# Batched 64x64 matmul: results stored in 1 KB runs, evacuations by partition halves, b loads ungated

## The chip, the cores and the metric

The kernel runs on one core of a Trainium2 chip. The metric is the device time of one execution in microseconds (us); each version ran several times, beside runs of the kernel before on the same chip. Engines: PE (TensorE, matmuls), DVE (VectorE), ACT (ScalarE), POOL (GpSimd, issues DMAs), SP (issues DMAs).

## The reference

```python
# a, b: 1024 x 64 x 64, float32, normal random numbers
def reference(a, b):
    return np.matmul(a, b).astype(np.float32)
```

50.3 MB go through memory (16.8 MB each for a, b and the result). The arithmetic is in bf16.

## The kernel before

Work goes in 16 **turns** t of 64 matrices. Tiles of a hold 128 matrices, so that a new one is prepared every second turn (s = t // 2).

```python
    b_v = b.rearrange("(t g h) (kp u) n -> t (h kp) g (u n)", h=4, g=16, u=2)
    o_v = out.rearrange("(t g h) (mo w) n -> t (h mo) g (w n)", h=4, g=16, w=2)
    # ... pools: 5 result tiles, 4 PSUM banks for results (o_psum, bufs=4), 4 for transposes

    def multiply(t):                       # cut
        for gq in range(4):
            o_ps = o_psum.tile([128, 4, 2, 64], fp32, name="o_ps")
            # ... 16 matmuls into o_ps
            if last and gq % 2:
                nc.vector.tensor_copy(o_sb[:, gq, :, :, :], o_ps[:])
            else:
                nc.scalar.copy(o_sb[:, gq, :, :, :], o_ps[:])

        # ... the loop, cut
        for t in range(n_t):
            s, half = t // 2, t % 2
            if t + 1 < n_t:
                spread(t + 1)              # DVE: 4 copies, transposed a -> block-diagonal weights
            if half == 0:
                if s + 2 < n_s:
                    regroup(s + 2)         # DVE: 1 copy, loaded a -> order for the transposes
                # ... load_a
            multiply(t)                    # PE matmuls, evacuation PSUM -> SBUF
            if t + 1 < n_t:
                cast(t + 1)                # ACT: b to bf16
            # ... load_b
            if half == 0 and s + 1 < n_s:
                transpose(s + 1, 1)        # PE transposes, then copies on DVE and ACT
            if half == 1 and s + 2 < n_s:
                transpose(s + 2, 0)
            # ... store(t - 1)
```

The order in which the program names operations is the order of each engine's queue: in the trace of this kernel DVE starts its 94 memsets, copies and casts, and ACT its 95 copies and casts, in just that order.

## Time and profile before

| | before |
|---|---|
| time, median | 138.62 us (138.28 to 138.86, 4 runs) |
| span of the profile | 137.0 us |

To read this: busy shares say which engine works, and the waits say for whom the others stand still. Here the compute engines have slack (DVE is busy for 62% of the span, ACT for 57%), and ACT waits 16.1 us for result buffers that DMA empties. The prediction below shows these lines.

### The profile page before, as it was taken

What the parts mean: (1) busy time and instruction counts of PE and PEld (TensorE: products, weight loads), DVE (VectorE), ACT (ScalarE), POOL (GpSimd) and SP (SyncE); (2) the same over time, 40 slices, a digit from 0 to 9 for tenths busy, and PEclk for the clock granted to TensorE, in tenths of its full rate; (3) what the DMA queues carried; (4) which work ended last, traced back from release to release, by engine and by line L of the source; (5) the groups of instructions that cost most, each with busy time, mean ns of one, the idle gap of its engine ahead of it and who ended that gap; (6) DMA issues with size and microseconds to landing.
All of it is one profiled execution on the core that took longest, in us unless ns stands there. A gap on an engine that the chain in (4) does not pass through costs nothing.

```text
span 137.0 us, 2995 instructions
## 1 busy us (share of the span) xinstructions
PE 58.8 (43%) x1280; PEld 56.7 (41%) x1280; DVE 85.2 (62%) x94; ACT 77.5 (57%) x98; POOL 43.3 (32%) x57
## 2 busy tenths in 40 slices
PE   0000810685339746843075800957019645508100
PEld 0000800685239746853075800956019645507100
DVE  5772573670999899999449850699207867904200
ACT  0103280199907999970889209791297999715100
POOL 6932211422723452333113443430030330232600
PEclk9999996599955999999559995599955999995955
DMA  2999999999999999999999999999999999999992
GB/s 18 184 297 306 305 306 306 301 274 262 243 271 270 316 359 274 272 356 383 340 276 273 379 374 331 271 289 383 377 383 384 378 382 383 376 386 368 301 278 90
DMA packets 17469, 42.14 MB, mean 308 GB/s; under 512 B 1072, under 2 KB 1072, under 8 KB 17456
## 3 DMA queue, kind: packets, MB, share of 16 engines
q0 software_dynamic: 9008, 25.17, 66.7%
q1 hardware_dynamic: 7392, 14.68, 30.4%
q10 hardware_dynamic: 1056, 2.10, 4.0%
q8 instruction: 10, 0.16, 0.5%
q14 instruction: 3, 0.02, 0.0%
HBM read 33.55 MB, written 16.78 MB: 367 GB/s over the span
## 4 chain that ended last, share of the span: by engine, by line
DMA 57%; issue 25%; POOL 11%; POOLq 1%
DMA a_sb<-in_a_dram 40%; DMA out_dram<-o_sb 18%; POOL out_dram L147 6%; POOL a_sb L65 3%; POOL out_dram L141 2%; POOLq L244 1%; POOL identity L178 0%; POOL identity L64 0%; POOLq L147 0%; POOLq L178 0%; POOLq L141 0%; POOLq L65 0%; POOLq L233 0%
## 5 line engine op out<-in xcount | busy, mean ns | idle before, releaser
L157 PE MATMUL o_ps<-b_bf,at_bd 128*128 128x64 bf16 x1024 | 40.4, 208 | 45.9 <-ACT b_bf L121 37.9
L115 DVE COPY at_bd<-at_sb 32x2048 bf16<-32x2048 bf16 x64 | 46.9, 733 | 20.5 <-ACT at_sb L105 19.5
L157 PEld LDWEIGHTS <-at_bd 128*128 128x128 bf16 x1024 | 39.8, 108 | 47.4 <-issue 35.6
L169 ACT COPY o_sb<-o_ps 128x512 f32<-128x512 f32 x62 | 33.5, 614 | 25.7 <-DMA out_dram<-o_sb 16.1
L65 POOL DMA_DIRECT2D a_sb<-in_a_dram x32 | 20.9, 667 | 41.0 <-DMA a_sb<-in_a_dram 30.2
L147 POOL DMA_DIRECT2D out_dram<-o_sb x15 | 18.8, 1253 | 40.3 <-ACT o_sb L169 27.6
L97 PE MATMUL at_ps<-identity,a_bf 128*128 128x128 bf16 x256 | 20.6, 246 | 22.7 <-DVE a_bf L88 22.7
L121 ACT CAST b_bf<-b_sb 128x2048 bf16<-128x2048 f32 x15 | 29.1, 1942 | 0.0
L97 PEld LDWEIGHTS <-a_bf 128*128 128x128 bf16 x256 | 18.1, 113 | 23.1 <-DVE a_bf L88 23.1
L105 ACT COPY at_sb<-at_ps 128x1024 bf16<-128x1024 bf16 x16 | 16.7, 1047 | 11.3 <-PE at_ps L97 11.3
L103 DVE COPY at_sb<-at_ps 128x1024 bf16<-128x1024 bf16 x16 | 19.5, 1222 | 3.9 <-PE at_ps L97 3.5
L88 DVE COPY a_bf<-a_sb 128x4096 bf16<-128x4096 bf16 x8 | 10.2, 1278 | 10.2 <-DMA a_sb<-in_a_dram 10.0
L177 DVE MEMSET at_bd<- 128x4096 uint32 x2 | 6.9, 3472 | 2.5 <-PEq L233 1.7
L105 ACT ACT_TABLE_LOAD x1 | 1.3, 1283 | 6.7 <-issue 6.7
L141 POOL DMA_DIRECT2D out_dram<-o_sb x4 | 3.0, 755 | 4.4 <-ACT o_sb L169 4.0
L167 DVE COPY o_sb<-o_ps 128x512 f32<-128x512 f32 x2 | 1.4, 692 | 2.7 <-PE o_ps L157 2.7
L128 ACT CAST b_bf<-b_sb 128x512 bf16<-128x512 f32 x2 | 1.1, 616 | 2.9 <-DMA b_sb<-in_b_dram 2.9
L126 DVE CAST b_bf<-b_sb 128x512 bf16<-128x512 f32 x2 | 0.8, 424 | 3.2 <-DMA b_sb<-in_b_dram 3.2
L73 ACT MOVE_SHAPE b_sb<-in_b_dram x2 | 0.6, 320 | 3.2 <-POOL identity L64 2.2
L178 POOL TENSOR_SCALAR_AFFINE_SELECT identity<-identity 128x128 bf16<-128x128 bf16 x1 | 0.3, 349 | 0.0
L64 POOL MEMSET identity<- 128x128 bf16 x1 | 0.2, 224 | 0.0
L233 POOL MEMSET const-float32-0.0<- 128x1 f32 x1 | 0.1, 99 | 0.2 <-issue 0.2
(3 smaller groups left out, 0.3 us busy)
## 6 DMA issues: line engine op xcount, KB each, us to landing
out_dram<-o_sb POOLq DMA_DIRECT2D x15, 1024.0 KB, 21.0
a_sb<-in_a_dram POOLq DMA_DIRECT2D x32, 256.0 KB, 18.0
out_dram<-o_sb POOLq DMA_DIRECT2D x4, 256.0 KB, 7.6
b_sb<-in_b_dram SPq DMA_DIRECT2D x14, 0.5 KB, 20.6
b_sb<-in_b_dram ACTq DMA_DIRECT2D x2, 0.5 KB, 21.7
```

Of the source, the lines that this page charges most:

```text
L65: nc.gpsimd.dma_start(out=a_sb[:, h, :, :].rearrange("p v k -> p (v k)"), in_=a_v[s, h])
L88: nc.vector.tensor_copy(a_bf[:], a_sb[:].rearrange("p h v k -> p v h k"))
L97: nc.tensor.transpose(at_ps[:, vo, :], a_cols[:, 2 * vo + w, u::2], identity[:])
L103: nc.vector.tensor_copy(dst, src)
L105: nc.scalar.copy(dst, src)
L115: nc.vector.tensor_copy(bd_v[rows, :, :, h, :], at_v[rows, :, half, :])
L121: nc.scalar.copy(b_bf[:], b_sb[:])
L141: nc.gpsimd.dma_start(out=o_v[t, :, 4 * gq : 4 * gq + 4, :], in_=o_sb[:, gq, :, :, :].rearrange("p g w n -> p (g w n)"),)
L147: nc.gpsimd.dma_start(out=o_v[t], in_=o_sb[:].rearrange("p q g w n -> p (q g w n)"))
L157: nc.tensor.matmul(o_ps[:, g4, w, :], at_bd[:, (2 * w + u) * 16 + g, :, :].rearrange("p h mo -> p (h mo)"), b_bf[:, g, 64 * u : 64 * u + 6 ...
L169: nc.scalar.copy(o_sb[:, gq, :, :, :], o_ps[:])
L177: nc.vector.memset(bd[:], 0.0)
```

## The change

The intent is to make the runs of the result in memory 1 KB long, where they were 512 B, so that its stores cost less DMA time. A result row of the matmul now holds two row halves (wl), and eight matrices share the 128 partitions. Evacuations (the copies that move matmul results from PSUM to SBUF) then have to move halves of the partitions, and they double in number. PSUM tiles of results double in size and halve in number. The second intent is to start b's first loads without waiting for a's first one.

```diff
-    o_v = out.rearrange("(t g h) (mo w) n -> t (h mo) g (w n)", h=4, g=16, w=2)
+    o_v = out.rearrange("(t gh x) (mo w) n -> t (x mo) gh (w n)", gh=8, x=8, w=4)
 ...
-        tc.tile_pool(name="o_psum", bufs=4, space=bass.MemoryType.PSUM)
+        tc.tile_pool(name="o_psum", bufs=2, space=bass.MemoryType.PSUM)
 ...  (load_b: the dependency on the first load of a is gone for t < 2)
 ...  (at_sb, at_bd: axes in another order, and spread's copies with them)
 ...  (transpose: each copy out of the transposes cut in two, one for each wl)
-        for gq in range(4):
-            o_ps = o_psum.tile([128, 4, 2, 64], fp32, name="o_ps")
 ...
-                nc.scalar.copy(o_sb[:, gq, :, :, :], o_ps[:])
+        def evacuate(o_ps, gh, gl, n):
+            for par in range(2):
+                for wl in range(2):
+                    src = o_ps[64 * wl : 64 * wl + 64, gl : gl + n, par, :, :]
+                    dst = o_sb[64 * par : 64 * par + 64, gh : gh + n, :, wl, :]
+                    if wl == par or (gh and not last):
+                        nc.scalar.copy(dst, src)
+                    else:
+                        nc.vector.tensor_copy(dst, src)
+        for half in range(2):
+            o_ps = o_psum.tile([128, 4, 2, 2, 64], fp32, name="o_ps")
 ...  (32 matmuls)
+                if last and g8 % 4 == 3:
+                    evacuate(o_ps, 4 * half + g8 // 4 * 2, g8 // 4 * 2, 2)
+            if not last:
+                evacuate(o_ps, 4 * half, 0, 4)
```

In the built program the four copies of a first half wait for each other. The semaphore values of turn 0:

```text
ACT  copy (par 0, wl 0)   waits PE  >= 80     then ACT counter = 8
DVE  copy (par 0, wl 1)   waits ACT >= 8
DVE  copy (par 1, wl 0)                       then DVE counter = 21
ACT  copy (par 1, wl 1)   waits DVE >= 21
```

I call this the **ring**. I read the values from the built program.

More of the change, by code (lines that the diff above doesn't have):

```diff
@@ L5 @@
 from concourse import bass_utils, mybir
+from concourse.masks import make_identity
 from concourse._compat import with_exitstack
@@ L49 @@
     o_psum = ctx.enter_context(
-        tc.tile_pool(name="o_psum", bufs=4, space=bass.MemoryType.PSUM)
+        tc.tile_pool(name="o_psum", bufs=2, space=bass.MemoryType.PSUM)
     )
     bd_tiles = [
-        consts.tile([128, 64, 4, 32], bf16, name=f"at_bd{i}") for i in range(N_BD)
+        consts.tile([128, 4, 16, 2, 4, 16], bf16, name=f"at_bd{i}") for i in range(N_BD)
     ]
@@ L57 @@
     a_tiles, b_tiles, abf_tiles, at_tiles, bbf_tiles = {}, {}, {}, {}, {}
-    held, begun = {}, []
+    held = {}
     def load_a(s):
@@ L62, in load_a @@
         for h in range(4):
-            if s == 0 and h == 1:
-                begun.append(nc.gpsimd.memset(identity[:], 0.0))
             nc.gpsimd.dma_start(
@@ L72, in load_b @@
         queue = nc.scalar if t in (1, 3) else nc.sync
-        load = queue.dma_start(out=b_sb[:], in_=b_v[t])
-        if t < 2:
-            tc.add_manual_dep(
-                load.ins,
-                begun[0].ins.name,
-                mybir.DependencyInfo(
-                    mybir.DependencyClass.Sync, mybir.DependencyReason.DATA
-                ),
-                reason="first load of a goes ahead",
-            )
+        queue.dma_start(out=b_sb[:], in_=b_v[t])
         b_tiles[t] = b_sb
@@ L89, in regroup, with transpose @@
         abf_tiles[s] = a_bf
-        at_tiles[s] = work.tile([128, 2, 2, 128, 8], bf16, name="at_sb")
-    def transpose(s, w):
+        at_tiles[s] = work.tile([128, 2, 2, 32, 2, 4, 4], bf16, name="at_sb")
+    def transpose(s, j):
         a_cols = abf_tiles[s][:].rearrange("p v h k -> p v (h k)")
         for u in range(2):
-            at_ps = t_psum.tile([128, 8, 128], bf16, name="at_ps")
-            for vo in range(8):
-                nc.tensor.transpose(
-                    at_ps[:, vo, :], a_cols[:, 2 * vo + w, u::2], identity[:]
-                )
-            dst = at_tiles[s][:, w, u, :, :]
-            src = at_ps[:].rearrange("p vo q -> p q vo")
-            if u == 0:
-                nc.vector.tensor_copy(dst, src)
-            else:
-                nc.scalar.copy(dst, src)
+            at_ps = t_psum.tile([128, 2, 4, 128], bf16, name="at_ps")
+            for wl in range(2):
+                for vo in range(4):
+                    nc.tensor.transpose(
+                        at_ps[:, wl, vo, :],
+                        a_cols[:, 4 * vo + 2 * j + wl, u::2],
+                        identity[:],
+                    )
+            src = at_ps[:].rearrange("p wl vo (g mp) -> p wl g mp vo", mp=4)
+            for wl in range(2):
+                dst = at_tiles[s][:, j, u, :, wl, :, :]
+                if u == 0:
+                    nc.vector.tensor_copy(dst, src[:, wl])
+                else:
+                    nc.scalar.copy(dst, src[:, wl])
     def spread(t):
-        at_v = at_tiles[t // 2][:].rearrange(
-            "p w u (g mp) vo -> p (w u) g (mp vo)", g=32
-        )
         half = slice(16 * (t % 2), 16 * (t % 2) + 16)
-        bd_v = bd_tiles[t % N_BD][:].rearrange("p (wu g) h mo -> p wu g h mo", g=16)
+        bd = bd_tiles[t % N_BD]
         for h in range(4):
             rows = slice(32 * h, 32 * h + 32)
-            nc.vector.tensor_copy(bd_v[rows, :, :, h, :], at_v[rows, :, half, :])
+            src = at_tiles[t // 2][rows, :, :, half, :, :, :].rearrange(
+                "p j u g wl mp vo -> p (j u) (g wl) (mp vo)"
+            )
+            dst = bd[rows, :, :, :, h, :].rearrange("p ju g wl mo -> p ju (g wl) mo")
+            nc.vector.tensor_copy(dst, src)
     def cast(t):
@@ L137, in multiply, with put @@
         last = t == n_t - 1
-        o_sb = o_pool.tile([128, 4, 4, 2, 64], fp32, name="o_sb")
-        def put(gq):
+        o_sb = o_pool.tile([128, 8, 2, 2, 64], fp32, name="o_sb")
+        def put(lo, n):
             nc.gpsimd.dma_start(
-                out=o_v[t, :, 4 * gq : 4 * gq + 4, :],
-                in_=o_sb[:, gq, :, :, :].rearrange("p g w n -> p (g w n)"),
-            )
-        def put_all():
-            nc.gpsimd.dma_start(
-                out=o_v[t], in_=o_sb[:].rearrange("p q g w n -> p (q g w n)")
-            )
-        for gq in range(4):
-            o_ps = o_psum.tile([128, 4, 2, 64], fp32, name="o_ps")
-            for g4 in range(4):
-                g = 4 * gq + g4
-                for w in range(2):
+                out=o_v[t, :, lo : lo + n, :],
+                in_=o_sb[:, lo : lo + n].rearrange("p gh j wl n -> p (gh j wl n)"),
+            )
+        def evacuate(o_ps, gh, gl, n):
+            for par in range(2):
+                for wl in range(2):
+                    src = o_ps[64 * wl : 64 * wl + 64, gl : gl + n, par, :, :]
+                    dst = o_sb[64 * par : 64 * par + 64, gh : gh + n, :, wl, :]
+                    if wl == par or (gh and not last):
+                        nc.scalar.copy(dst, src)
+                    else:
+                        nc.vector.tensor_copy(dst, src)
+        for half in range(2):
+            o_ps = o_psum.tile([128, 4, 2, 2, 64], fp32, name="o_ps")
+            for g8 in range(8):
+                g = 8 * half + g8
+                for j in range(2):
                     for u in range(2):
                         nc.tensor.matmul(
-                            o_ps[:, g4, w, :],
-                            at_bd[:, (2 * w + u) * 16 + g, :, :].rearrange(
-                                "p h mo -> p (h mo)"
+                            o_ps[:, g8 // 2, g8 % 2, j, :],
+                            at_bd[:, 2 * j + u, g, :, :, :].rearrange(
+                                "p wl h mo -> p (wl h mo)"
                             ),
@@ L165, in multiply @@
                         )
-            if last and gq % 2:
-                nc.vector.tensor_copy(o_sb[:, gq, :, :, :], o_ps[:])
-            else:
-                nc.scalar.copy(o_sb[:, gq, :, :, :], o_ps[:])
-        held[t] = [lambda q=q: put(q) for q in range(4)] if last else [put_all]
+                if last and g8 % 4 == 3:
+                    evacuate(o_ps, 4 * half + g8 // 4 * 2, g8 // 4 * 2, 2)
+            if not last:
+                evacuate(o_ps, 4 * half, 0, 4)
+        if last:
+            held[t] = [lambda q=q: put(2 * q, 2) for q in range(4)]
+        else:
+            held[t] = [lambda: put(0, 8)]
     with tc.manual_schedule():
@@ L177 @@
             nc.vector.memset(bd[:], 0.0)
-        nc.gpsimd.affine_select(
-            out=identity[:],
-            in_=identity[:],
-            compare_op=mybir.AluOpType.not_equal,
-            fill=1.0,
-            base=0,
-            pattern=[[-1, 128]],
-            channel_multiplier=1,
-        )
+        make_identity(nc, identity)
         for s in range(1, A_AHEAD):
```

## The prediction

> **What bounds the kernel now.** I read the page's head first, then the DMA view of a late stretch, then the waits, then the timeline of ScalarE (ACT).
>
> The page: busy time by engine, and the 40 slices in tenths (clock and DMA).
>
> ```profile
> PE 58.8 (43%) x1280; PEld 56.7 (41%) x1280; DVE 85.2 (62%) x94; ACT 77.5 (57%) x98; POOL 43.3 (32%) x57
> ...
> PEclk9999996599955999999559995599955999995955
> DMA  2999999999999999999999999999999999999992
> ```
>
> No compute engine reaches two thirds, while the 16 DMA engines are full from the second slice to the last but one. The clock falls to 5 or 6 after pauses of TensorE (PE).
>
> The DMA view of 90 to 120 us (packets, MB, share of the 16 engines), when only b and results move:
>
> ```profile
> q0 software_dynamic: 1960, 7.27, 66.9%
> q1 hardware_dynamic: 1959, 3.90, 35.6%
> ```
>
> Results (q0) and b (q1) together take 102%: both queues always have work. Results cost 0.669 x 30 x 16 / 7.27 = 44 engine-us per MB, so all 16.8 MB cost 16.8 x 44 / 16 = 46 us of the span. That is the time the change goes after.
>
> The waits (us, times, longest):
>
> ```profile
> PE o_ps L157 <- ACT b_bf L121: 37.9, 13, 7.7
> ...
> POOL out_dram L147 <- ACT o_sb L169: 27.6, 7, 9.4
> ...
> ACT o_sb L169 <- DMA out_dram<-o_sb: 16.1, 3, 5.9
> ```
>
> PE waits for ACT's cast of b, ACT in its turn for result buffers to leave by DMA. So compute has slack and gives it back to DMA. How fast compute goes when nothing holds it shows in ACT's timeline (start, us, operation):
>
> ```profile
> 46.75 2.06 ACT L169 COPY o_sb<-o_ps 128x512 f32<-128x512 f32 x4
> 48.66 1.95 ACT L121 CAST b_bf<-b_sb 128x2048 bf16<-128x2048 f32 x1
> 50.46 1.07 ACT L105 COPY at_sb<-at_ps 128x1024 bf16<-128x1024 bf16 x1
> 51.37 2.11 ACT L169 COPY o_sb<-o_ps 128x512 f32<-128x512 f32 x4
> 53.28 2.00 ACT L121 CAST b_bf<-b_sb 128x2048 bf16<-128x2048 f32 x1
> ```
>
> One turn (64 matrices) takes 51.37 - 46.75 = 4.6 us, all of it ACT. DMA needs about 130 / 16 = 8.1 us per turn. The **slack is some 3.5 us per turn**; a change that makes a turn longer than about 8 us moves the bound from DMA to compute.
>
> [...]
> - [...] its 4096 B packets of results, eight runs each, took 174 ns in the median[...].
> - [...] no copy overtakes another on DVE or ACT. My prediction rests on this.
> - [...] The trace has 692 ns, which I use. [...]
> - [...] The trace has 2.03 us for the 64 matmuls of a turn after short gaps, and 3.57 us after gaps of 3.7 us and over.
>
> **The change part by part.** The rows used:
>
> ```profile
> L115 DVE COPY at_bd<-at_sb 32x2048 bf16<-32x2048 bf16 x64 | 46.9, 733 | 20.5 <-ACT at_sb L105 19.5
> ...
> L169 ACT COPY o_sb<-o_ps 128x512 f32<-128x512 f32 x62 | 33.5, 614 | 25.7 <-DMA out_dram<-o_sb 16.1
> L121 ACT CAST b_bf<-b_sb 128x2048 bf16<-128x2048 f32 x15 | 29.1, 1942 | 0.0
> ...
> L88 DVE COPY a_bf<-a_sb 128x4096 bf16<-128x4096 bf16 x8 | 10.2, 1278 | 10.2 <-DMA a_sb<-in_a_dram 10.0
> ...
> L167 DVE COPY o_sb<-o_ps 128x512 f32<-128x512 f32 x2 | 1.4, 692 | 2.7 <-PE o_ps L157 2.7
> ```
>
> 1. Results in 1 KB runs: [...]
> 2. b ungated: its first packet came at about 6 us, but loads of a filled the DMA engines from 4 us on. About 0, and a's first tiles may come half a microsecond later.
> 3. Evacuations: a turn had four copies of 128x512. It now has eight of 64x512, each as long. Six are on ACT: 2 x 0.48 us more from start to start. Two are on DVE: 2 x 0.69 = 1.4 us.
> 4. Copies out of the transposes are cut in two: about 0.05 us more per turn on ACT and 0.15 us on DVE[...].
> 5. By busy time alone DVE would then need about 2.8 (spread) + 0.6 (half a regroup) + 1.4 + 1.4 = 6.2 us per turn, and ACT 0.48 x 6 + 1.8 + 1.0 = 5.7 us. Both are under 8.1 us. If that were all, DMA would stay the bound.
>
> That isn't all. **The order decides.** In the compiled program the four copies of a first half wait in a ring: ACT's first copy, then DVE's two (they wait for ACT's semaphore after it), then ACT's second, which waits for the DVE semaphore value that only DVE's second copy sets. I can't tell from the program whether the shared PSUM tile or the interleaved writes to one result tile cause this; the waits are there either way. DVE's pair stands behind the spread of the next turn and, every second turn, a regroup. ACT's second copy stands in front of the four copies of the second half, the cast for the next turn and the copies out of the transpose. Before, DVE was in this loop only through the spread, well ahead of its use.
>
> The new loop, counted from D, the end of DVE's pair in a turn:
> - ACT: one copy and four more, 5 x 0.48 = 2.4, then the cast, 1.95: the next turn's matmuls start at D + 4.4.
> - Half of them: 1.0 us warm, 1.8 cold (half of 2.03 or 3.57). With some 5 us of idle PE per turn I take cold, as in the trace after such pauses: D + 6.2.
> - ACT's first copy 0.6, DVE's pair 1.4: the next D is **8.2 us** later, if DVE was free. After odd turns it is: copies 1.4, spread 2.8, regroup 1.2, together 5.4.
> - After even turns it isn't. The spread for the next tile of a needs ACT's copies out of the transposes, which stand behind the cast: D + 2.4 + 1.8 + 1.1 = 5.3. Spread 2.8, pair 1.4: **9.5 us**.
>
> Two turns: 17.7 us, and with some 0.2 us per turn for passing semaphores[...] about 18.1, so **9.05 us per turn against DMA's 8.1**. DMA loses the bound[...].
>
> The sum: the pair of turn 0 stands behind the regroup of the third tile of a, which ran from 33.9 to 35.1 us (it waits for a's load): D(0) = 36.5. Seven pairs of turns: D(14) = 36.5 + 7 x 18.1 = 163. Then ACT's five copies 2.4, first cast piece 0.6, matmuls 3.6, the last quarter's ring of four shorter copies 1.6, store issue 0.8[...]: 175. The last landing before was at 136.2 and the time 138.76, so 2.6 more: **about 177 us**, and I put it at 176 for some turns with a warm clock.
>
> **The rivals.**
> - A: DMA stays the bound. The ring would have to cost less than 8 us a turn, as when copies on both engines overlapped. [...] The full DMA slices speak for it; the semaphore values of the program speak against it.
> - B: the ring, but a warm PE: 0.8 us less in every odd turn, 5 to 6 us in all: 170. PE's idle time of some 5 us a turn speaks against it.
> - C: the ring, and slower DVE copies. The spread now writes runs of 16 elements in place of 32, and each 0.1 us per copy adds 0.4 us to each even turn, 2.8 us in all. The DVE copies that move partitions may cost more as well. 180 to 186. No row of before has such a copy, so I leave it in the upper range.
>
> **Range and chances.** B's end and some overlap that I missed give 167, C's end 187. A has about one chance in twenty, split around the border of 2%: faster 0.03, same 0.03, slower 0.94.
>
> **What would show it.** Right: DMA slices well under 9 from the middle on;[...] the largest waits those of ACT's evacuation on DVE's and of DVE's on the spread; matmul bursts 8 to 9.5 us apart, alternating; ACT and DVE both idle a third of the time. Step by step: the evacuation rows near 600 ns (ACT) and 690 ns (DVE) at half the partitions, the spread near 730 ns. Wrong: full DMA slices to the end[...], or evacuations of the two engines that overlap in time.

Passages are cut where marked. In the sum one term is cut, some 3 us for the landing of the last store: the terms from D(14) = 163 on came to 175 us with it and come to 172 without, and with the last 2.6 to the about 177 and the 176 that stand there. What can be measured of this:

- The last 256 KB store of the changed kernel landed 2.5 us after its issue (182.63 to 185.16 us), the median of its four too.
- The last landing in the trace of before is at 135.8 us. 136.2 is what the last issue (128.6 us) and the median of the page (7.6 us) add up to.
- Cold and warm: the burst of 3.57 us at 85.9 us ran at a granted clock of 0.50, those of 2.03 us at 46.0 and 50.7 us at 1.00.
- The 692 ns are those of DVE's copy of 128x512 out of PSUM (row L167). That 64x512 lasts as long was an assumption; the changed kernel shows it: 688 ns on DVE, and 579 on ACT against 614 before.
- Part 4 can be had from the trace of before: two starts of 0.48 us against one of 0.91 on ACT, two copies of 0.69 us against one of 1.22 on DVE.
- The 0.2 us per turn for passing semaphores is an estimate. In the trace of before DVE started 0.03 us after the ACT copy that it waited for, ACT 0.04 us after PE, and PE 0.05 to 0.06 us after ACT or DVE.
- The four shorter copies of the last ring took 2 x 0.37 us on ACT and 2 x 0.42 on DVE in the changed kernel.

## The result and the profile after

| | before | after |
|---|---|---|
| time, median | 138.62 us | 189.00 us (188.71 to 189.16, 4 runs) |
| ratio | | 1.363 (1.360 to 1.367) |
| span of the profile | 137.0 us | 186.6 us |

A ratio is the mean time of one kernel's fast runs over that of the other's of the same rounds, so not quite the ratio of the medians. The result is correct. The time lies 2 us above the stated range.

The page of the changed kernel, busy time and DMA in 40 slices:

```profile
PE 80.2 (43%) x1280; PEld 77.9 (42%) x1280; DVE 107.8 (58%) x146; ACT 103.7 (56%) x150; POOL 37.5 (20%) x57
...
DMA  4999999999999999799989387948795506060731
```

DVE has 22.6 us more work and ACT 26.2, yet each stands still for over two fifths of the span. DMA is full in the first half only. So **no engine is the bound: a chain of waits is**.

Its waits (us in total, times, longest):

```profile
PE o_ps L159 <- ACT b_bf L117: 68.8, 14, 6.8
ACT o_sb L149 <- DVE o_sb L151: 38.3, 19, 3.6
DVE at_bd L111 <- ACT at_sb L100: 31.0, 8, 4.7
DVE o_sb L151 <- ACT o_sb L149: 26.1, 11, 4.7
```

L149 and L151 are the evacuations on ACT and DVE. They wait for each other, 64 us together, and none of these waits existed before. ACT's wait for result buffers to leave (16.1 us before) is gone.

Two turns on ACT (start, us, operation, idle time before it and its releaser):

```profile
64.34 2.94 ACT L149 COPY o_sb<-o_ps 64x512 f32<-64x512 f32 x5 [3.04 <-DVE o_sb L151]
67.31 1.90 ACT L117 CAST b_bf<-b_sb 128x2048 bf16<-128x2048 f32 x1
69.23 1.07 ACT L100 COPY at_sb<-at_ps 128x512 bf16<-128x512 bf16 x2
71.16 0.58 ACT L149 COPY o_sb<-o_ps 64x512 f32<-64x512 f32 x1 [0.86 <-PE o_ps L159]
73.20 2.94 ACT L149 COPY o_sb<-o_ps 64x512 f32<-64x512 f32 x5 [1.46 <-DVE o_sb L151]
...
83.61 2.94 ACT L149 COPY o_sb<-o_ps 64x512 f32<-64x512 f32 x5 [3.01 <-DVE o_sb L151]
```

and the same stretch on DVE:

```profile
62.92 1.39 DVE L151 COPY o_sb<-o_ps 64x512 f32<-64x512 f32 x2
...
65.64 2.78 DVE L111 COPY at_bd<-at_sb 32x2048 bf16<-32x2048 bf16 x4
68.45 1.48 DVE L79 COPY a_bf<-a_sb 128x4096 bf16<-128x4096 bf16 x1
71.77 1.39 DVE L151 COPY o_sb<-o_ps 64x512 f32<-64x512 f32 x2 [1.84 <-ACT o_sb L149]
...
79.19 2.96 DVE L111 COPY at_bd<-at_sb 32x2048 bf16<-32x2048 bf16 x4 [4.64 <-ACT at_sb L100]
82.18 1.39 DVE L151 COPY o_sb<-o_ps 64x512 f32<-64x512 f32 x2
```

Follow the ring once round. DVE's pair ends at 64.31. At 64.34 ACT starts its five copies; the cast follows at 67.31 and the matmuls of the next turn at 69.26. ACT's first copy comes at 71.16, and DVE's next pair runs to 73.16: a turn of 8.85 us. Now the next one: ACT's copies out of the transposes end at 79.16 (78.09 + 1.07). Only then may DVE spread, at 79.19, and its pair ends at 83.57: a turn of **10.41 us**. In this second turn ACT sits idle for 3 us with its data ready, because DVE's pair stands behind the spread in DVE's queue.

The last turn has a ring in each quarter. PE there (start, us):

```profile
172.44 1.01 PE L159 MATMUL o_ps<-b_bf,at_bd 128*128 128x64 bf16 x16 [4.08 <-ACT b_bf L124]
175.20 1.86 PE L159 MATMUL o_ps<-b_bf,at_bd 128*128 128x64 bf16 x32 [1.74 <-ACT o_sb L149]
179.63 1.01 PE L159 MATMUL o_ps<-b_bf,at_bd 128*128 128x64 bf16 x16 [2.57 <-ACT o_sb L149]
```

The matmuls of the second and fourth quarter wait until the quarter before them in the same PSUM tile has been evacuated: 1.7 and 2.6 us.

### The profile page after: what moved, and what is told of

It reads as the page before. It is cut to its first block, busy times and chain, and to the rows that moved or that the text cites. A ratio compares the mean times of both kernels' runs of the same rounds, so it can differ in the third digit from the quotient of the medians.

```text
span 186.6 us, 3100 instructions
## 1 busy us (share of the span) xinstructions
PE 80.2 (43%) x1280; PEld 77.9 (42%) x1280; DVE 107.8 (58%) x146; ACT 103.7 (56%) x150; POOL 37.5 (20%) x57
## 4 chain that ended last, share of the span: by engine, by line
ACT 35%; DVE 24%; issue 20%; PE 8%; DMA 7%; POOL 2%; POOLq 0%; DVEq 0%
ACT o_sb L149 17%; ACT b_bf L117 14%; DVE at_bd L111 11%; DVE o_sb L151 10%; DMA a_sb<-in_a_dram 7%; PE o_ps L159 6%; ACT at_sb L100 5%; PE at_ps L89 2%; DVE a_bf L79 2%; POOL out_dram L137 2%; POOL a_sb L65 1%; POOLq L241 0%; DVE at_sb L98 0%; POOLq L137 0%; DVEq L79 0%
## 5 line engine op out<-in xcount | busy, mean ns | idle before, releaser
L159 PE MATMUL o_ps<-b_bf,at_bd 128*128 128x64 bf16 x1024 | 56.7, 239 | 77.2 <-ACT b_bf L117 68.8
L159 PEld LDWEIGHTS <-at_bd 128*128 128x128 bf16 x1024 | 55.8, 129 | 79.1 <-issue 70.5
L149 ACT COPY o_sb<-o_ps 64x512 f32<-64x512 f32 (+1 forms) x98 | 55.1, 562 | 55.1 <-DVE o_sb L151 38.3
L137 POOL DMA_DIRECT2D out_dram<-o_sb x19 | 18.4, 971 | 126.9 <-ACT o_sb L149 116.6
L151 DVE COPY o_sb<-o_ps 64x512 f32<-64x512 f32 (+1 forms) x38 | 24.0, 632 | 26.6 <-ACT o_sb L149 26.1
L89 PE MATMUL at_ps<-identity,a_bf 128*128 128x128 bf16 x256 | 26.1, 284 | 23.3 <-DVE a_bf L79 23.3
L89 PEld LDWEIGHTS <-a_bf 128*128 128x128 bf16 x256 | 23.4, 133 | 23.5 <-DVE a_bf L79 23.5
L100 ACT COPY at_sb<-at_ps 128x512 bf16<-128x512 bf16 x32 | 17.2, 589 | 17.2 <-PE at_ps L89 16.9
L98 DVE COPY at_sb<-at_ps 128x512 bf16<-128x512 bf16 x32 | 20.6, 686 | 5.6 <-PE at_ps L89 5.3
L65 POOL DMA_DIRECT2D a_sb<-in_a_dram x32 | 18.4, 592 | 18.6 <-DMA a_sb<-in_a_dram 16.4
```

The costliest lines, as they stand in the source:

```text
L65: nc.gpsimd.dma_start(out=a_sb[:, h, :, :].rearrange("p v k -> p (v k)"), in_=a_v[s, h])
L89: nc.tensor.transpose(at_ps[:, wl, vo, :], a_cols[:, 4 * vo + 2 * j + wl, u::2], identity[:],)
L98: nc.vector.tensor_copy(dst, src[:, wl])
L100: nc.scalar.copy(dst, src[:, wl])
L137: nc.gpsimd.dma_start(out=o_v[t, :, lo : lo + n, :], in_=o_sb[:, lo : lo + n].rearrange("p gh j wl n -> p (gh j wl n)"),)
L149: nc.scalar.copy(dst, src)
```

## The experiments

**My theory:** the ring, which ties DVE's queue order into ACT's, makes the loop of a turn longer than DMA's 8 us. **Rivals:** the doubled copies simply fill the engines; or the start, with b ahead of a, costs the time. Besides, I wanted to know why the loop was longer than I had reckoned, and what the 1 KB runs are worth. The runs were made on several chips; the kernel before took 138.6 to 138.9 us on each, so times of different chips are compared.

| run | time, median (us) | kernel before, same chip (us) |
|---|---|---|
| act_first | 155.56 (fast run 151.96) | 138.72 |
| by_tile | 154.80 | 138.94 |
| pair_early | 176.35 | 138.72 |
| cast_early | 164.13 | 138.72 |
| full_rows (wrong result) | 177.38 | 138.72 |
| gated | 190.56 | 138.72 |
| before_ungated | 138.79 | 138.72 |
| order_and_cast | 141.89 | 138.72 |
| order_cast_ungated | 139.36 | 138.72 |
| cast_early_to_14 | 139.25 | 138.82 |
| cast_early_hold_1 | 139.44 | 138.82 |

### act_first: ACT's two copies ahead of DVE's two

```diff
-            for par in range(2):
-                for wl in range(2):
+            for par, wl in ((0, 0), (1, 1), (0, 1), (1, 0)):
+                if True:
```

> The same copies, only their order in a first half changed: ScalarE's two first, then VectorE's two, so ScalarE no longer waits for VectorE within a turn. If the ring is the cause, the loop falls from 9.6 us a turn to what is left without VectorE in it: half the matmuls 1.9, the rest 1.8, four copies 2.4, cast 1.9, together 8.0 us with a cold clock (14 turns x 1.65 = 23 us less, about 165 us), and about 6.5 us with a warm one, where DMA with its 8 us a turn takes over (138 to 145 us). Rival, the added copy work itself fills the engines: the work is the same, so 186 to 190 us.

Measured: 152.0 to 156.8 us, with the same copies on the same engines. The runs scatter; only the 151.96 us run counts as fast, the other three as slow by the rule of 1.5%, though their granted clock was no lower (0.747 to 0.762 against 0.742). The distance to 189 us is many times that scatter. From the profile of a slow run (156.8 us), ACT:

```profile
60.66 1.17 ACT L149 COPY o_sb<-o_ps 64x512 f32<-64x512 f32 x2 [0.73 <-PE o_ps L159]
62.36 2.36 ACT L149 COPY o_sb<-o_ps 64x512 f32<-64x512 f32 x4 [0.53 <-PE o_ps L159]
64.74 1.90 ACT L117 CAST b_bf<-b_sb 128x2048 bf16<-128x2048 f32 x1
...
68.60 1.17 ACT L149 COPY o_sb<-o_ps 64x512 f32<-64x512 f32 x2 [0.98 <-PE o_ps L159]
```

ACT waits for PE alone, and a turn takes 7.9 us here (68.60 - 60.66), between 7.2 and 7.9 along the stretch I looked at. That the full work fits into 152 to 157 us rules out the first rival: the work alone is worth at most 13 to 18 of the 50 us. (What makes up these 13 to 18 is not separated: the doubled copies, or the larger PSUM tiles, which ACT can begin to empty only after 32 matmuls, 1.90 us (69.26 to 71.16) in the changed kernel, and not after 16, 1.05 us (85.91 to 86.96) before.) My two cases, cold and warm clock, were too clean: matmul bursts took 2.7 to 3.6 us, between the two (2.03 and 3.57 us in the kernel before), and the time fell between them too.

### by_tile: each PSUM tile evacuated by one engine

```diff
-                    if wl == par or (gh and not last):
+                    if gh >= 4:
```

> The changed kernel with each PSUM tile evacuated by one engine: the four copies of a first half all on VectorE, those of a second half on ScalarE as before. No PSUM tile is shared, and in the built program neither engine waits for the other's copies. VectorE has two copies more per turn (1.4 us), ScalarE two fewer (1.2). If the ring is what costs, the loop is matmuls 3.6, four copies 2.4, cast 1.9, about 7.9 us cold: 189 - 14 x 1.7 = 165 us, 155 to 168, less where the clock is warm. If VectorE's load were the matter (it grows from 6.2 to 7.6 us a turn), the time would rise above 189 us.

Measured: 154.8 us (153.9 to 156.0), a ratio of 1.113 to the kernel before. This is at the lower edge of the expected 155 to 168. DVE got **more** work, and the time fell by 34 us. Two different ways to open the ring lead to the same time.

Where do the ring's waits come from? I also built, without running it, a version in which DVE's pair writes to an SBUF tile of its own. The same waits for the values 8 and 21 stood in it. That speaks for the shared PSUM tile and against the interleaved writes. Taking just these waits away is no experiment: the scheduling layer sets them, and by_tile and act_first take away what makes them instead.

### pair_early: the ring kept, DVE's pair ahead of the spread

```diff
+            multiply(t)
             if t + 1 < n_t:
                 spread(t + 1)
             ...  (regroup, load_a)
-            multiply(t)
```

> The ring stays, but VectorE's pair of a turn stands ahead of the spread and the regroup in VectorE's queue. If the queue order makes the long turns (10.4 us against 8.85), every turn takes 8.85 us: 7 x 1.55 = 11 us less, about 178 us. If the ring's own copies are all that counts, both kinds of turn stay and so does 189 us.

Measured: 176.35 us, 12.7 us less than 189.0. ACT's five copies, each time just after DVE's pair:

```profile
68.11 2.95 ACT L149 COPY o_sb<-o_ps 64x512 f32<-64x512 f32 x5 [1.46 <-DVE o_sb L151]
...
76.97 2.95 ACT L149 COPY o_sb<-o_ps 64x512 f32<-64x512 f32 x5 [1.46 <-DVE o_sb L151]
...
85.84 2.95 ACT L149 COPY o_sb<-o_ps 64x512 f32<-64x512 f32 x5 [1.46 <-DVE o_sb L151]
```

Every turn now takes 8.86 us. The long turns were long because of the queue order, and with DVE's pair ahead of the spread the ring takes 8.86 us.

### cast_early: the ring kept, the cast ahead of the evacuations

```diff
+            if t + 1 < n_t:
+                cast(t + 1)
             multiply(t)
-            if t + 1 < n_t:
-                cast(t + 1)
```

> The changed kernel with its ring, but ScalarE casts b for the next turn ahead of the turn's evacuations. If the loop runs over the cast as I say (ring, five copies, cast, matmuls), the cast leaves the path between the ring and the next matmuls, and the loop is ScalarE's own sum with its wait for VectorE: about 8.0 to 8.4 us a turn, so 189 - 14 x 1.4 = 169 us, 164 to 172. If the ring alone sets the pace, whatever stands behind it, 186 to 190 us.

Measured: 164.13 us, in the range. The matmuls no longer stand behind evacuation and cast in a row; the loop is what I said it is. In its profile PE waits for evacuations to free PSUM tiles (55.1 us in 31 waits) and no longer for the cast (68.8 us in the changed kernel), and the five copies start 7.8 and 8.3 us apart in turn.

### full_rows: the same number of copies over all partitions (wrong result)

```diff
-                    src = o_ps[64 * wl : 64 * wl + 64, gl : gl + n, par, :, :]
-                    dst = o_sb[64 * par : 64 * par + 64, gh : gh + n, :, wl, :]
+                    src = o_ps[:, gl : gl + n, par, :, :]
+                    dst = o_sb[:, gh : gh + n, :, wl, :]
```

> Wrong result on purpose: the same number of evacuating copies with the same free size, each over all 128 partitions, so that none starts at partition 64. In the changed kernel ScalarE's copies follow each other at 0.59 us and at 0.48 in the kernel before. If the changing start partition is the reason, the spacing returns to 0.48, five copies and the cast take 0.55 us less and the copies after the cast start 0.1 us earlier: 0.6 us x 15 turns, about 180 us. If the waits for VectorE or the doubled number of copies are the reason, the spacing stays at 0.59 and the time at 189 us.

Measured: 177.38 us, 2.6 us less than expected. ACT:

```profile
70.22 2.54 ACT L149 COPY o_sb<-o_ps 128x512 f32<-128x512 f32 x5 [1.35 <-DVE o_sb L151]
72.62 1.94 ACT L117 CAST b_bf<-b_sb 128x2048 bf16<-128x2048 f32 x1
74.42 1.12 ACT L100 COPY at_sb<-at_ps 128x512 bf16<-128x512 bf16 x2
```

Five copies and the start of the cast take 2.40 us (72.62 - 70.22) where the changed kernel takes 2.97 (67.31 - 64.34). The cast's successor starts 1.80 us after it, not 1.92. The number of copies and the waits are the same (ACT waited 19 times for DVE's evacuations and DVE 11 times for ACT's, in both). So it is the **half-partition form of the copies that takes away the overlap of neighbours on ACT**: each lasts about as long (0.58 and 0.60 us), but starts only when the one before it has ended (0.59 us apart, 2.97 / 5, and 0.48 with full partitions, 2.40 / 5). DVE's pair shrinks too, from 1.39 to 1.29 us. The changing start partition is my reading. The trace of cast_early speaks for it and against the number of partitions:

```profile
63.37 1.91 ACT L117 CAST b_bf<-b_sb 128x2048 bf16<-128x2048 f32 x1
65.17 0.58 ACT L149 COPY o_sb<-o_ps 64x512 f32<-64x512 f32 x1
```

Here a copy of 64 partitions that reads and writes from partition 0 starts 0.11 us before the cast over all 128 has ended (63.37 + 1.91 = 65.28). The evacuating copies that do not overlap all read or write another half than their neighbour. But one pair does not fit: the cast and the copies out of the transposes cover all 128 partitions, and in the changed kernel they do not overlap (67.31 + 1.90 = 69.21, next start 69.23). So what exactly takes the overlap away stays open.

### gated and before_ungated: the start

`gated` puts the dependency for b's first loads back into the changed kernel; `before_ungated` takes it out of the kernel before.

> The changed kernel with the first loads of b held back until the first load of a is issued, as before. The first tile of a should be back near 12.8 us (16.8 in the changed kernel) and the first matmuls near 26.7 us (28.5). The third tile of a then lands later, near 33.9 us, so that the pair of turn 0 ends near 36 us where it ended at 34.7: 187 to 191 us. If the ungated loads cost the start what the first tile lost, 4 us, it is 185 us.

> The kernel before with the first loads of b ungated, nothing else. The first tile of a should come about 4 us later (near 16.8 us where it was 12.8), as in the changed kernel. DMA was full from 4 us on in the kernel before and b's bytes only change places with a's, so with DMA as the bound the time should stay within 1 us of 138.7. If the late first tile costs what it is late, 142 us.

Measured: 190.56 us (1.6 us more than the changed kernel, other chip) and 138.79 us (ratio 1.0005, 0.9981 to 1.0029). Ungated, the first tile of a is ready 3.5 us later (regroup at 16.8 us against 13.3 gated), but the third one is ready earlier, and DVE's pair of turn 0 ends at 34.7 us against 36.5. In the kernel before, where DMA is the bound, taking the gate out is worth nothing. The second rival falls: the ungated start costs nothing here.

### Both orders at once: can the change win?

`order_and_cast` has act_first, the cast early but for the last two turns, the gate, and the last turn evacuated by halves. `order_cast_ungated` is the same without the gate. `cast_early_to_14` (from the ungated one) casts early in turn 14's place too, and `cast_early_hold_1` also stores each turn in its own turn.

> Both orders at once (ScalarE's two copies first; the cast ahead of the evacuations but for the last two turns), b gated as before, and the last turn evacuated by halves in place of quarters. No loop over both engines is left: ScalarE's sum is 6 copies x 0.59 + cast 1.9 + 1.1 = 6.5 us a turn, VectorE's 6.2, both under DMA's 8. DMA should be the bound again, and the 1 KB runs show their worth: packets of results took 165 ns in full stretches of the changed kernel against 174, 5% of 46 us = 2.4 us, so 136 to 138 us. If compute still loses 8 us somewhere at the start or the end, 140 to 146 us.

> The same without the gate for b: within 2 us of the gated one, in either direction, since b's and a's first bytes only change places.

> The ungated version with both orders, and the cast ahead of the evacuations in the last but one turn too. There the matmuls of turn 14 waited until 118.4 us for a cast that stood behind the copies of turn 13. They should start some 2 us earlier, and with them the stores of the last two turns: 137 to 139 us, the kernel before being 138.7. If the end hangs on the landing of the last b (122.3 us) alone, no change: 139.4 us.

> The same with each turn's result stored in its own turn and not one turn later. The stores stand behind their copies in any case, so within 1 us of the version without it, unless stores issued earlier in GpSimd's queue hold back loads of a behind them: then 1 to 3 us more.

Measured: 141.89 (a miss: 136 to 138 expected), 139.36 (a miss too: within 2 us of the gated one expected), 139.25 and 139.44 us, ratios of 1.022, 1.006, 1.005 and 1.005. The 50 us are gone, but none beats the kernel before. Here the gate does cost something, 2.5 us: with it the matmuls of turn 1 start at 36.5 us against 34.6, and the last ones at 128.4 against 125.1. Compute has little slack left to make up a late start; that this is the reason is a reading of the two traces and not tested. The last two small edits changed nothing that can be told from the scatter.

Here DMA is full again from 5 to 120 us (1.06 to 1.08 of the 16 engines in the windows), and the 1 KB runs can be weighed. The stretch must hold b and results alone. The prediction's 90 to 120 us does not quite: until 93.5 us the last 131 packets of a are among those of q0, 2 KB each at 172 ns. The DMA view of 95 to 120 us, of the kernel before:

```profile
q0 software_dynamic: 1623, 6.25, 66.9%
q1 hardware_dynamic: 1619, 3.22, 35.1%
```

and of order_cast_ungated:

```profile
q0 software_dynamic: 1687, 6.50, 67.5%
q1 hardware_dynamic: 1675, 3.32, 34.7%
```

Results cost 0.669 x 25 x 16 / 6.25 = 42.8 engine-us per MB before and 0.675 x 25 x 16 / 6.50 = 41.5 here, 3% less: 1.3 us of the span. In the trace's packet records of this stretch the median packet of results fell from 174 to 169 ns. That of b fell from 89 to 85 ns, though b's runs are as they were; no run says why. Both together moved 381 GB/s before and 395 here.

And where is the gain? The two windows at the end, 120 to 130 and 130 to 137 us (busy us of PE, PEld, DVE, ACT, POOL with counts, then clock, DMA share, GB/s), of the kernel before:

```profile
120.00:130.00 10.00, 3.40 (x64) 3.38 (x64) 2.16 (x5) 2.67 (x5) 4.17 (x5) 0.83 1.02 354
130.00:137.00 7.00, 0.00 (x0) 0.00 (x0) 0.00 (x0) 0.00 (x0) 0.00 (x0) 0.53 0.61 183
```

and of order_cast_ungated:

```profile
120.00:130.00 10.00, 5.03 (x102) 4.80 (x99) 4.52 (x8) 6.93 (x12) 1.30 (x2) 0.67 0.77 286
130.00:137.00 7.00, 0.00 (x0) 0.00 (x0) 0.73 (x2) 0.00 (x0) 2.42 (x4) 0.50 0.44 152
```

DMA stands idle for 10 x 0.23 + 7 x 0.56 = 6.2 us of the end, of which 0.6 us lie behind the end of the span at 136.4 us, against 2.7 us before. DVE and ACT are busy for over 91 of the 100 us from 20 to 120 (71 and 70 before). The last matmuls start at 125.1 us (124.0 before), and the last two stores are issued from 131.3 us on, where the kernel before issued its last at 128.6. So compute comes late with the last turn and DMA runs dry; what the longer runs save seems to be given back there. This is read from the traces, not shown by a run: cast_early_to_14 was meant to bring turn 14 forward, but its matmuls then waited until 119.2 us for DVE to free their PSUM tile (118.4 us without the edit).

## Why the prediction was right or wrong

**Right:** the direction, the reason and the shape. The ring sets the pace, DMA loses the bound, the turns alternate, and DVE's copies stand where they were said to stand. act_first and by_tile show it by taking the ring away, pair_early and cast_early by moving one part of it each. A (DMA stays the bound) fell with the DMA row. B (a warm clock) fell: bursts of a turn took 3.2 to 3.6 us, and a warm one took 2.03 before. C's slower spread did not come: 695 ns on average, less than before (733; but four copies took 2.96 us in the long turns, where 2.8 was reckoned). DVE's pair, whose copies move partitions, took the 1.4 us that it was given (1.39).

**Wrong:** the size, 189 us against 176 (its terms add up to 177.8, not 177) and a range up to 187. The step that failed is the term "5 x 0.48 = 2.4" of the loop, five copies on ACT up to the cast: I took the spacing of 128-partition copies for copies of half the partitions. It measured 2.97 us. Its sister, the "+ 1.8" from the cast to the copies after it, measured 1.92 us; these operations cover all partitions, and with the evacuating copies in the order of act_first it was 1.81 (66.55 - 64.74), so why it grew stays open. Together they lengthen the short turn by about 0.6 us and the long one by 0.7, and the two turns took 19.2 us on average where the prediction had 18.1. full_rows shows the first: with full partitions DVE's pairs end 8.23 and 9.48 us apart, 17.7 us for two turns, the sum that the prediction had before its allowance for semaphores. That the time of full_rows, 177.4 us, is close to the predicted one too is luck: against it the prediction's start is 1.7 us late, its seven pairs of turns 2.7 us long and its end 4.0 us short.

The rest of the account, from the profile of the changed kernel (a run of 188.7 us):

| term | prediction | measured | difference |
|---|---|---|---|
| end of DVE's pair in turn 0 | 36.5 | 34.7 | -1.8 |
| seven times two turns | 126.7 | 134.1 | +7.4 |
| from there to the time (with the 3 us of landing, cut above) | 14.6 | 19.9 | +5.3 |
| sum | 177.8 | 188.7 | +10.9 |

The third row is a second, smaller error; either error alone would have left the sum under 187 us: the last turn was reckoned as matmuls with one quarter's ring behind them, but PE waits 4.3 us for the ring of the quarter before in the same PSUM tile. The first row: ungating was put at "about 0" and half a microsecond for a's first tile. It was 3.5 us for that tile and an earlier third tile.

The gain from the 1 KB runs could not show in the changed kernel. Where it can show, in order_cast_ungated, it is 3% per MB (42.8 to 41.5 engine-us), and the median packet took 169 ns where it took 174 before. The prediction had put it higher; that rested on no trace. Two readings of lines were off as well: 90 to 120 us held some packets of a, so results cost 42.8 engine-us per MB and not 44, and the slow bursts before took 3.4 to 3.6 us, not always 3.57.

## What to carry to other kernels

When two engines share the evacuation of one PSUM tile, look for the waits that the built program puts between their copies, and ask what stands ahead of each copy in its engine's queue: here two reordered lines were worth over 30 us without a copy more or less. Before trading DMA time for copies, reckon the loop of a turn through all queues, not the busy time by engine, which fitted well below DMA's pace here (6.2 and 5.7 us per turn in the forecast against 8.1). And take a duration and the spacing of neighbours as two numbers: a new shape can keep the first and lose the second, as ACT's copies did here (0.60 us and 0.48 apart with 128 partitions, 0.58 us and 0.59 apart with halves).
